# Chunk heads of a hybrid streaming encoder: one running minimum over both parts of the scores, and transposed probabilities laid out from a pair's first key block on

## Chip, cores and metric

One Trainium2 chip, one core. The metric is the device time of one execution in microseconds (us); several runs give a median. Engines: PE is TensorE, DVE is VectorE, ACT is ScalarE, POOL is GpSimd, SP is SyncE, whose queue here starts every transfer (DMA).

## What is computed

A step of two layers over 1024 prompt tokens and 64 sample tokens (T = 1088). Each layer normalizes the input, projects it, mixes tokens in three branches (latent attention with 8 heads, pooling, chunk attention with 4 heads), merges the branches, and applies an output projection and a gated side input. The change touches the chunk attention, whose core in the reference is:

```python
def ca_attend(q, k, v, q_pos, k_pos, rel_table):
    s = jnp.einsum("bnqhd,bnkhd->bnhqk", q, k).astype(jnp.float32) * CA_HEAD_DIM ** -0.5
...
    s = jnp.where(mask[None, :, None], s + bias[None], NEG_INF)
    pr = jax.nn.softmax(s, axis=-1).astype(v.dtype)
    return jnp.einsum("bnhqk,bnkhd->bnqhd", pr, v)
```

A query of a 64-token chunk sees its own chunk and the 8 before it, with a bias that depends on the distance.

## The kernel before

All matrices are multiplied in single precision split into a high and a low part (`mm3`: three matmuls for one product). Each layer runs in stages: projection (`gemm`, lines 349 to 395), attention (`attn_phase`, 759), a final merge (1423), output projection and gate (again `gemm`). The attention takes 12 heads in the order of `HEADS`: the 4 chunk heads, then the 8 latent heads. A head has 9 units, one for each block of 128 queries (`qb` 0 to 7 of the prompt, 8 is the sample). Chunk heads go through them in the order 8, 0, 1, ... 7.

`attention` (732) emits the units as a pipeline: scores of unit i, then the transposes, exponential, normalization and PV matmuls of earlier units. Beside them it emits filling work that needs nothing of the attention: `ple_proj` (1381; 16 steps a layer, each of which stores a tile `o` to `pp`), the pooling branch (1250) and `merge_bc` (1353; it loads the branch outputs `mbo` and `o`). A scheduler then sets the order of the instructions on each engine by its own estimate of when each is ready, so a shorter chain in one place moves the filling work of all engines and the transfers on SP's queue. Each engine runs its queue in that order.

A chunk unit (961) has up to 5 key blocks of 128. With over 512 score columns (`qb` 4 to 7: 640; the sample: 576) the scores are made in `nb = 2` parts, each in its own PSUM bank. One DVE instruction per part (line 986, shown in the profile as CUSTOM_DVE_ANT_0 with a DVE_READ_ACCUMULATOR2_ANT behind it, in the orders as ISA) adds the bias, negates, writes the result to `P` in SBUF and leaves the part's minimum in a column of `st`. `softmax` (796) then takes the minimum of both columns (line 803), ACT makes the exponential with it as its bias and the sum of the row (807), DVE the reciprocal (814) and POOL the multiplication (815). The latent units (1031) have their own minimum per part (1059) and use the same `softmax`, where the minimum of line 803 stays.

`transp` (832) transposes up to four blocks of `P` on PE into one PSUM bank and copies them into tiles `PT` of four key blocks, for a pair of query blocks: each copy (`split`) is an ACT cast (line 108) and a DVE subtraction (119). Before, the tile of key block b is `b // 4`, so a group of four transposed blocks that does not start at a multiple of 4 needs two copies. `weigh` (853) multiplies the values with them on PE (875; 867 for the sample).

Of the kernel before, what the change touches and what calls it, by code (L numbers as in the profile page):

```python
# [10 lines left out]
F32 = mybir.dt.float32  # L11
# [62 lines left out]
class K:  # L74
# [721 lines left out]
    def softmax(self, u, s, n, nb, st):  # L796

        nc = self.nc
        if not hasattr(u, "p"):
            u.p = self.sp.tile([128, 1024], F32, tag="P", name="P", bufs=NP)  # L800
        w = n // len(s)
        if nb == 2:
            nc.vector.tensor_tensor(st[:, 0:1], st[:, 0:1], st[:, 1:2], op=ALU.min)

        def exp():
            for c, x in enumerate(s):
                nc.scalar.activation(u.p[:, c * w:c * w + w], x, AF.Exp, bias=st[:, 0:1], scale=-1.0,  # L807
                                     accum_out=st[:, 2 + c:3 + c])
        u.exp = exp

        def norm():
            if len(s) == 2:
                nc.vector.tensor_add(st[:, 2:3], st[:, 2:3], st[:, 3:4])
            nc.vector.reciprocal(st[:, 4:5], st[:, 2:3])  # L814
            nc.gpsimd.tensor_scalar(u.p[:, :n], u.p[:, :n], st[:, 4:5], 1.0, op0=ALU.mult, op1=ALU.mult)  # L815
        u.norm = norm

    def unit(self, u, blocks, n, grp, qb, order, v, o, r0, z, dst):

        samp = qb == 8  # L820
        cols = [min(128 * i, n - 128) for i in range(len(blocks))]
        u.last = samp or qb % 2 == 1
        u.transposes = lambda i: self.transp(u.p, blocks[i:i + 4], cols[i:i + 4], grp, samp, qb % 2)

        def weigh():
            c0, w = (1024, 64) if samp else (256 * (qb // 2), 256)
            self.weigh(grp, v, o(), r0, c0, w)
            if r0:
                self.gated(o(), c0, w, qb // 2 == order[0] // 2, qb == order[-1], z, dst)
        u.weigh = weigh  # L830

    def transp(self, p, bb, cols, grp, samp, half):

        if not bb:
            return
        nc = self.nc
        w = 64 if samp else 128
        o = 0 if samp else 128 * half
        ps = self.pn.tile([128, 4, 128], F32, tag="n", name="pT")
        for j, c0 in enumerate(cols):  # L840
            nc.tensor.transpose(ps[:, j], p[:, c0:c0 + 128], self.ident)  # L841
        for b in bb:
            if b // 4 not in grp:
                grp[b // 4] = self.sp.tile([128, 4, 2, 256], F32R, tag="PT", name="PT", bufs=NPT)
            grp.setdefault("have", {}).setdefault(b, set()).add(half)
        j = 0
        while j < len(bb):
            m = min(len(bb) - j, 4 - bb[j] % 4)
            t = grp[bb[j] // 4][:, bb[j] % 4:bb[j] % 4 + m]
            self.split(ps[:, j:j + m, 128 - w:], t[:, :, 0, o:o + w], t[:, :, 1, o:o + w], "a", "v")  # L850
            j += m

    def weigh(self, grp, v, o, r0, c0, w):

        nc = self.nc
        have = grp["have"]
        if w == 256:
            for b, hs in have.items():
                if len(hs) == 1:
                    z = 128 * (1 - next(iter(hs)))  # L860
                    nc.gpsimd.memset(grp[b // 4][:, b % 4, :, z:z + 128].bitcast(F32), 0.0)
        ps = self.pv.tile([128, 512], F32, tag="v", name="pv")
        bl = sorted(have)
        t = self.sp.tile([128, 512], F32, tag="ot", name="ot", bufs=2)
        if w == 64:
            for i, b in enumerate(bl):
                nc.tensor.matmul(ps[:, :128].rearrange("p (j w) -> p j w", j=2), lhsT=v(b), rhs=grp[b // 4][:, b % 4, :, :w],
                                 start=i == 0, stop=i == len(bl) - 1)
            nc.scalar.copy(t[:64, :128], ps[64:, :128])
            nc.vector.tensor_add(t[:64, :128], ps[:64, :128], t[:64, :128])  # L870
            nc.vector.tensor_add(o[r0:r0 + 64, c0:c0 + w], t[:64, :64], t[:64, 64:128])
            return
        for i, b in enumerate(bl):
            for j in range(2):
                nc.tensor.matmul(ps[:, :w], lhsT=v(b), rhs=grp[b // 4][:, b % 4, j, :w], start=i + j == 0,  # L875
                                 stop=i == len(bl) - 1 and j == 1)
        self.npv = getattr(self, "npv", -1) + 1
        if PVE[self.npv % len(PVE)] == "v":
# [82 lines left out]
    def chunk_unit(self, p, h, qb, grp):  # L961
# [12 lines left out]
        def scores():  # L974
# [5 lines left out]
            for c in range(nb):  # L980
                ps = self.pg.tile([128, 512], F32, tag="s", name="S")
                cc = slice(c * w, c * w + w)
                for q in (q1, q2):
                    nc.tensor.matmul(ps[:, :w], lhsT=q[:, q0:q0 + 128], rhs=k[:, k0 + c * w:k0 + c * w + w],
                                     start=q is q1, stop=q is q2)
                nc.vector.tensor_tensor_reduce(out=u.p[:, cc], in0=ps[:, :w], in1=b[:, cc], op0=ALU.add, scale=-1.0,
                                               scalar=3e38, op1=ALU.min, accum_out=st[:, c:c + 1])
            self.softmax(u, [u.p[:, :n]], n, nb, st)
        u.scores = scores
        return u  # L990
# [642 lines left out]
```

## Time and profile before

| | |
|---|---|
| median of 3 runs | 2325.16 us |
| runs | 2326.8, 2313.66, 2325.16 us |
| profiled execution | 2322.09 us |
| its span, first to last instruction | 2320.2 us |
| instructions | 44847 |
| mean granted TensorE clock | 0.963 of full speed |
| chunk heads, layer 0 | about 590 to 697 us |
| chunk heads, layer 1 | about 1738 to 1846 us |

The span is one execution as the profiler saw it; the profiled execution's own time is 1.9 us longer. A row's time is the busy time of that group; "idle before" is how long the engine had nothing to do just before, with the one it waited for. The duration of an instruction is counted from where the engine takes it up, so two in a row can overlap in the records by some 0.07 us.

### The profile page before, as it was taken

The page shows a single profiled execution, that of the slowest core. Times are in us where ns is not written, and L with a number is a line of the kernel's source. Part 1 is how long each engine was busy: PE and PEld are TensorE (multiplying, and loading weights), DVE is VectorE, ACT ScalarE, POOL GpSimd, SP SyncE. Part 2 cuts the span into 40 slices and gives each one's busy share as a digit, 9 for nine tenths or more (in the row PEclk, how much of TensorE's full clock was granted, in tenths as well). Part 3 has the DMA queues.
Part 4 walks back from the last instruction along what each step waited for, and adds up shares of the span by engine and source line. Part 5 has one row for each costly group of instructions (what it writes and reads, how often), then busy time and mean ns, then how long its engine had stood idle before and what let it go on. Part 6 is the DMA issues. An engine that isn't in the chain of part 4 may idle for free.

```text
span 2320.2 us, 44847 instructions
## 1 busy us (share of the span) xinstructions
PE 2164.3 (93%) x16134; PEld 2081.4 (90%) x16134; DVE 1804.3 (78%) x3620; ACT 1211.6 (52%) x2549; POOL 908.8 (39%) x1048
## 2 busy tenths in 40 slices
PE   5999999999789999998979999999998899999988
PEld 4999999999688998998969999999987789999988
DVE  8566778766578888989996667877746788889898
ACT  6334355554577666345553343555546676654452
POOL 0444545576455554000004354447564565530000
PEclk8999999999899999998979999999998999999989
DMA  3533456454976764554634344453569666645353
GB/s 127 179 109 124 162 165 185 132 153 140 270 206 176 196 175 142 194 195 143 200 108 152 116 146 168 150 178 121 161 173 265 194 187 178 187 173 194 131 172 124
DMA packets 222193, 385.81 MB, mean 166 GB/s; under 512 B 30404, under 2 KB 114196, under 8 KB 221972
## 3 DMA queue, kind: packets, MB, share of 16 engines
q1 hardware_dynamic: 221972, 382.95, 52.8%
q8 instruction: 129, 2.11, 0.4%
q14 instruction: 92, 0.75, 0.1%
HBM read 248.16 MB, written 134.70 MB: 165 GB/s over the span
## 4 chain that ended last, share of the span: by engine, by line
PE 62%; DVE 15%; DMA 11%; issue 5%; ACT 4%; POOL 3%; SPq 1%; POOLq 0%; DVEq 0%; ACTq 0%
PE g L366 42%; PE S L1055 3%; DMA pp<-o 3%; PE pv L875 3%; PE pT L841 3%; DMA K<-bias_p 1%; DVE wop L119 1%; DMA g<-z 1%; PE mps L130 1%; PE mps L132 1%; PE mps L131 1%; SPq L85 1%; PE vps L1024 1%; DVE S L331 1%; PE turn L1100 1%
## 5 line engine op out<-in xcount | busy, mean ns | idle before, releaser
L108 ACT CAST wop<-wraw 128x512 fp32r<-128x512 f32 (+1 forms) x230 | 138.9, 606 | 266.0 <-PE g L366 171.3
L635 POOL TENSOR_TENSOR z<-z,rbc 128x544 f32<-128x544 f32 x134 | 206.7, 1547 | 180.9 <-DVE z L634 164.8
L815 POOL TENSOR_SCALAR P<-P,st 128x640 f32<-128x640 f32 (+8 forms) x216 | 155.3, 723 | 198.9 <-DVE st L814 116.6
L108 ACT CAST wop<-S 128x512 fp32r<-128x512 f32 x234 | 144.9, 619 | 165.8 <-PE g L366 163.8
L119 DVE TENSOR_TENSOR wop<-S,wop 128x512 fp32r<-128x512 f32 x194 | 170.1, 877 | 76.5 <-ACT wop L108 75.8
L119 DVE TENSOR_TENSOR PT<-pT,PT 128x512 fp32r<-128x512 f32 (+4 forms) x360 | 167.7, 473 | 47.5 <-ACT PT L108 45.4
L119 POOL TENSOR_TENSOR wop<-wraw,wop 128x512 fp32r<-128x512 f32 (+1 forms) x112 | 148.1, 1324 | 120.8 <-ACT wop L108 120.4
L366 PE MATMUL g<-T1h,wop 128*128 128x272 f32 x960 | 181.5, 301 | 14.2 <-DVE U L374 13.8
L366 PE MATMUL g<-B11h,wop 128*128 128x272 f32 x960 | 175.7, 293 | 18.1 <-ACT B11h L110 13.5
L366 PE MATMUL g<-T3h,wop 128*128 128x272 f32 x960 | 178.0, 294 | 13.3 <-ACT T3h L108 13.3
L366 PE MATMUL g<-T2h,wop 128*128 128x272 f32 x960 | 178.1, 295 | 5.6 <-ACT T2h L108 5.6
L366 PE MATMUL g<-B21h,wop 128*128 128x272 f32 x960 | 177.4, 295 | 5.8 <-ACT P L378 5.8
L108 ACT CAST PT<-pT 128x512 fp32r<-128x512 f32 (+4 forms) x360 | 147.1, 420 | 57.7 <-PE pT L841 50.6
L366 PE MATMUL g<-T4h,wop 128*128 128x272 f32 x960 | 173.8, 293 | 0.3 <-DVE U L374 0.3
L366 PE MATMUL g<-B22h,wop 128*128 128x272 f32 x960 | 172.9, 290 | 0.0
L875 PE MATMUL pv<-PT,V 128*128 128x256 f32 x928 | 167.6, 300 | 2.0 <-DVE PT L119 1.2
L1055 PE MATMUL S<-K,Q 96*128 96x384 f32 (+5 forms) x672 | 159.1, 353 | 7.5 <-ACT P L807 7.4
L366 PEld LDWEIGHTS g<-T1h,wop 128*128 128x128 f32 x960 | 148.5, 199 | 16.2 <-issue 13.8
L841 PE MATMUL pT<-ident,P 128*128 128x128 f32 x936 | 159.4, 280 | 2.8 <-DVE PT L119 1.5
L366 PEld LDWEIGHTS g<-B11h,wop 128*128 128x128 f32 x960 | 143.0, 192 | 20.5 <-ACT B11h L110 13.5
L130 PE MATMUL mps<-oh,wop 128*128 128x272 f32 x512 | 154.9, 304 | 5.6 <-ACT oh L108 3.2
L366 PEld LDWEIGHTS g<-T3h,wop 128*128 128x128 f32 x960 | 145.1, 193 | 15.6 <-ACT T3h L108 15.0
(269 smaller groups left out, 6509.0 us busy)
## 6 DMA issues: line engine op xcount, KB each, us to landing
wraw<-win SPq DMA_DIRECT2D x88, 512.0 KB
z<-z SPq DMA_DIRECT2D x96, 272.0 KB
g<-z SPq DMA_DIRECT2D x64, 272.0 KB
z<-z SPq DMA_DIRECT2D x24, 544.0 KB
Q<-q SPq DMA_DIRECT2D x32, 408.0 KB
K<-k SPq DMA_DIRECT2D x32, 400.0 KB
k<-hl SPq DMA_DIRECT2D x48, 256.0 KB
q<-hl SPq DMA_DIRECT2D x64, 192.0 KB
```

Of the source, the lines that this page charges most:

```text
L85: self.nc.sync.dma_start(out=self.raw(out), in_=self.raw(in_))
L108: nc.scalar.copy(out, src)
L119: e.tensor_sub(out, src, hi)
L130: mm(ps, lhsT=wh, rhs=xh, start=first, stop=False)
L131: mm(ps, lhsT=wh, rhs=xl, start=False, stop=False)
L132: mm(ps, lhsT=wl, rhs=xh, start=False, stop=last)
L366: nc.tensor.matmul(ps[:, c, :C], lhsT=hl[:, w, kb, :], rhs=b[:, kb, c * C:(c + 1) * C], start=k == 0 and not more, stop=k == 11, skip_grou ...
L635: nc.gpsimd.tensor_mul(o, o, self.half(self.r, ti))
L815: nc.gpsimd.tensor_scalar(u.p[:, :n], u.p[:, :n], st[:, 4:5], 1.0, op0=ALU.mult, op1=ALU.mult)
L841: nc.tensor.transpose(ps[:, j], p[:, c0:c0 + 128], self.ident)
L875: nc.tensor.matmul(ps[:, :w], lhsT=v(b), rhs=grp[b // 4][:, b % 4, j, :w], start=i + j == 0, stop=i == len(bl) - 1 and j == 1)
L1055: nc.tensor.matmul(ps[:, :ww], lhsT=q[0:96, q0:q0 + 128], rhs=k[0:96, k0 + c * w:k0 + c * w + ww], start=i == 0, stop=i == 2 and not diag)
```

## The change

In a chunk unit with two parts, the second part's reduction starts from the minimum of the first (a column of `st`, read as one number per partition) instead of from 3e38, and leaves the minimum of both in column 0. The separate minimum of line 803 stays for the latent units alone. And the tiles `PT` of a pair are counted from the first key block of the pair's first unit, with the groups of transposes cut so that each lies in one tile. The core of the diff:

```diff
@@ softmax
-        if nb == 2:
+        if len(s) == 2:
             nc.vector.tensor_tensor(st[:, 0:1], st[:, 0:1], st[:, 1:2], op=ALU.min)
@@ unit
-        u.transposes = lambda i: self.transp(u.p, blocks[i:i + 4], cols[i:i + 4], grp, samp, qb % 2)
+        m = grp.setdefault("first", blocks[0])
+        k = min(4, 4 - (blocks[0] - m) % 4)
+        u.transposes = lambda i: self.transp(u.p, *((x[k:] if i else x[:k]) for x in (blocks, cols)), grp, samp, qb % 2)
@@ transp
+        m = grp["first"]
         for b in bb:
-            if b // 4 not in grp:
-                grp[b // 4] = self.sp.tile([128, 4, 2, 256], F32R, tag="PT", name="PT", bufs=NPT)
+            if (b - m) // 4 not in grp:
+                grp[(b - m) // 4] = self.sp.tile([128, 4, 2, 256], F32R, tag="PT", name="PT", bufs=NPT)
...
         while j < len(bb):
-            m = min(len(bb) - j, 4 - bb[j] % 4)
-            t = grp[bb[j] // 4][:, bb[j] % 4:bb[j] % 4 + m]
-            self.split(ps[:, j:j + m, 128 - w:], t[:, :, 0, o:o + w], t[:, :, 1, o:o + w], "a", "v")
-            j += m
+            i = (bb[j] - m) % 4
+            k = min(len(bb) - j, 4 - i)
+            t = grp[(bb[j] - m) // 4][:, i:i + k]
+            self.split(ps[:, j:j + k, 128 - w:], t[:, :, 0, o:o + w], t[:, :, 1, o:o + w], "a", "v")
+            j += k
@@ weigh
-        have = grp["have"]
+        have, m = grp["have"], grp["first"]
+
+        def at(b):
+            return grp[(b - m) // 4][:, (b - m) % 4]
...
@@ chunk_unit
                 nc.vector.tensor_tensor_reduce(out=u.p[:, cc], in0=ps[:, :w], in1=b[:, cc], op0=ALU.add, scale=-1.0,
-                                               scalar=3e38, op1=ALU.min, accum_out=st[:, c:c + 1])
+                                               scalar=st[:, 1:2] if c else 3e38, op1=ALU.min,
+                                               accum_out=st[:, 1:2] if c < nb - 1 else st[:, 0:1])
```

Elsewhere in `weigh` the tiles are looked up by `at(b)`; nothing else changes. Latent heads begin with key block 0 in every unit of the prompt, so their groups stay as they were. Lines from 824 on move down by up to 9.

DVE, layer 0, the last units of the first chunk head (`ISA P,st` is the reduction of line 986, `ISA st` its accumulator read, `S` the scores, `K` the bias in a tile of that name). Before:

```order
L986 ISA P,st<-S,K_6856 128x320
L986 ISA st 128x1
L986 ISA P,st<-S,K_6856 128x320
L986 ISA st 128x1
L119 TENSOR_TENSOR PT<-pT,PT 128x4x128
L814 RECIPROCAL st<-st 128x1
L803 TENSOR_TENSOR st<-st 128x1
```

and now:

```order
L994 ISA P,st<-S,K_6856 128x320
L994 ISA st 128x1
L814 RECIPROCAL st<-st 128x1
L888 TENSOR_TENSOR o<-pv,ot 64x256
L119 TENSOR_TENSOR PT<-pT,PT 128x4x128
L994 ISA P,st<-S,K_6856,st 128x320
L994 ISA st 128x1
```

The second reduction now names `st` as an input, stands behind three other instructions, and nothing of line 803 follows it. It waits for DVE's own semaphore of the first part, as line 803 did.

ACT, layer 0, copies of transposed probabilities between the second and the third chunk head (`PT<-pT` is the cast, `o<-pps` a copy of `ple_proj`, `ot<-pv` one of the PV output). Before:

```order
L108 CAST PT<-pT 128x128 x2
L807 ACTIVATE P,st<-P,st 128x128
L1394 COPY o<-pps 128x272
L108 CAST PT<-pT 128x2x128
L879 COPY ot<-pv 64x256
L108 CAST PT<-pT 128x128
L108 CAST PT<-pT 128x2x128
```

and now:

```order
L108 CAST PT<-pT 128x2x128
L807 ACTIVATE P,st<-P,st 128x128
L1403 COPY o<-pps 128x272
L108 CAST PT<-pT 128x4x128
L887 COPY ot<-pv 64x256
L108 CAST PT<-pT 128x128
```

Two casts of one block became one of two, and two of two blocks one of four.

SP, layer 0, transfers before the last chunk head (`pp<-o` is a store of `ple_proj`, `V<-vc` a load of values). Before:

```order
L85 DMA wraw<-wpp 128x2x128
L85 DMA pp_107<-o 128x544
L85 DMA V<-vc_125 128x1664
```

and now:

```order
L85 DMA wraw<-wpp 128x2x128
L85 DMA V<-vc_125 128x1664
L85 DMA pp_107<-o 128x544
```

The store stands behind the load. Further on, among the first latent heads, the store `mbo<-po` and the loads `of<-mbo` and `of<-o` of `merge_bc` stand some places later than before.

## Rows read from the trace of the kernel before

**Rows 1.** The page, part 1: busy time, share of span, instructions of each engine.

```profile
PE 2164.3 (93%) x16134; PEld 2081.4 (90%) x16134; DVE 1804.3 (78%) x3620; ACT 1211.6 (52%) x2549; POOL 908.8 (39%) x1048
```

**Rows 2.** Stretches: length, busy PE, PEld, DVE, ACT, POOL (instructions); clock, DMA share, GB/s.

```profile
590.00:697.00 107.00, 88.20 (x571) 78.86 (x571) 73.09 (x262) 70.05 (x199) 54.30 (x86) 0.90 0.84 233
697.00:740.00 43.00, 37.61 (x255) 32.29 (x254) 34.25 (x97) 30.12 (x87) 25.50 (x34) 0.99 0.77 219
740.00:950.00 210.00, 206.47 (x1576) 193.22 (x1575) 178.93 (x483) 131.51 (x373) 93.64 (x133) 0.99 0.58 170
...
1738.00:1846.00 108.00, 87.19 (x567) 77.97 (x568) 73.21 (x262) 71.14 (x201) 54.19 (x86) 0.90 0.83 232
```

**Rows 3.** Chain of waits within 590 to 697 us, then 1738 to 1846 us, by line.

```profile
by line: DMA pp<-o 35.4%; DMA K<-bias_p 13.8%; DMA of<-p 6.1%; SPq L85 5.6%; PE pv L875 4.7%; PE S L984 4.5%; PE pps L130 4.2%; PE pT L841 3.8%; DVE P L986 3.2%; PE pps L131 2.7%; PE pps L132 2.6%; issue 2.6%; PE vps L1024 2.5%; DVE st L803
...
by line: DMA pp<-o 27.0%; DMA K<-bias_p 8.5%; DMA z<-z 5.4%; PE pT L841 5.2%; DMA pu<-z 5.0%; PE pv L875 4.9%; DVE P L986 4.9%; PE S L984 4.7%; PE pps L130 4.2%; issue 3.8%; SPq L85 3.2%; PE pps L131 3.1%; PE pps L132 3.0%; PE vps L1024 2.5
```

**Rows 4.** ACT's waits, the same two stretches: us in total, times, longest.

```profile
ACT o L1394 <- DMA pp<-o: 10.2, 4, 3.3
...
ACT P L807 <- DVE st L803: 3.9, 3, 2.0
...
ACT o L1394 <- DMA pp<-o: 14.2, 5, 6.5
ACT P L807 <- DVE st L803: 4.5, 4, 1.9
```

**Rows 5.** Line 803: both stretches (length, DVE busy), then all 120, ns min/median/max.

```profile
590.00:697.00 107.00, 6.78 (x19) 0.90 0.84 233
1738.00:1846.00 108.00, 6.63 (x19) 0.90 0.83 232
...
L803 DVE TENSOR_TENSOR st<-st x120: 128/154/1790, 598.7 to 2059.8; 128x1 f32<-128x1 f32 x120
```

**Rows 6.** In order of time, DVE, then POOL: start, duration in us.

```profile
660.84 0.08 DVE L986 DVE_READ_ACCUMULATOR2_ANT st<- 128x1 f32 x1
660.84 0.49 DVE L986 CUSTOM_DVE_ANT_0 P<-S,K 128x320 f32<-128x320 f32 x1
...
661.92 1.79 DVE L803 TENSOR_TENSOR st<-st 128x1 f32<-128x1 f32 x1
...
661.87 0.73 POOL L891 TENSOR_TENSOR o<-o,acc 128x256 f32<-128x256 f32 x1
662.57 1.11 POOL L1275 TENSOR_TENSOR pb<-pa 128x560 f32<-128x560 f32 x1
```

**Rows 7.** In order of time, DVE, line 803 without POOL in its way.

```profile
635.66 0.15 DVE L803 TENSOR_TENSOR st<-st 128x1 f32<-128x1 f32 x1
635.73 0.15 DVE L814 RECIPROCAL st<-st 128x1 f32<-128x1 f32 x1
```

**Rows 8.** Line 1107 (ns min/median/max), one instance in time, POOL beside it.

```profile
L1107 DVE SCALAR_TENSOR_TENSOR hl<-turn,gh,hl x26: 471/736/751, 330.6 to 1542.0; 128x512 fp32r<-128x512 f32 x24, 128x256 fp32r<-128x256 f32 x2
...
333.76 0.73 DVE L1107 SCALAR_TENSOR_TENSOR hl<-turn,gh,hl 128x512 fp32r<-128x512 f32 x1
...
333.31 1.36 POOL L635 TENSOR_TENSOR z<-z,rbc 128x544 f32<-128x544 f32 x1 [3.94 <-DVE z L634]
```

**Rows 9.** Copies of transposed probabilities, 590 to 697 us: busy us, mean ns, idle before.

```profile
L119 DVE TENSOR_TENSOR PT<-pT,PT 128x128 fp32r<-128x128 f32 x22 | 5.7, 281 | 1.4 <-ACT PT L108 1.4
L119 DVE TENSOR_TENSOR PT<-pT,PT 128x384 fp32r<-128x384 f32 x10 | 5.5, 550 | 0.6 <-ACT PT L108 0.4
...
L108 ACT CAST PT<-pT 128x128 fp32r<-128x128 f32 x22 | 5.2, 265 | 0.4
L108 ACT CAST PT<-pT 128x384 fp32r<-128x384 f32 x10 | 4.7, 472 | 1.3 <-PE pT L841 1.3
```

**Rows 10.** Transfers issued from 590 to 700 us: the loads of values, size each.

```profile
V<-vc SPq DMA_DIRECT2D x4, 832.0 KB
```

More of the change, by code (lines that the diff above doesn't have):

```diff
@@ L860, in weigh @@
                     z = 128 * (1 - next(iter(hs)))
-                    nc.gpsimd.memset(grp[b // 4][:, b % 4, :, z:z + 128].bitcast(F32), 0.0)
+                    nc.gpsimd.memset(at(b)[:, :, z:z + 128].bitcast(F32), 0.0)
         ps = self.pv.tile([128, 512], F32, tag="v", name="pv")
@@ L866, in weigh @@
             for i, b in enumerate(bl):
-                nc.tensor.matmul(ps[:, :128].rearrange("p (j w) -> p j w", j=2), lhsT=v(b), rhs=grp[b // 4][:, b % 4, :, :w],
+                nc.tensor.matmul(ps[:, :128].rearrange("p (j w) -> p j w", j=2), lhsT=v(b), rhs=at(b)[:, :, :w],
                                  start=i == 0, stop=i == len(bl) - 1)
@@ L874, in weigh @@
             for j in range(2):
-                nc.tensor.matmul(ps[:, :w], lhsT=v(b), rhs=grp[b // 4][:, b % 4, j, :w], start=i + j == 0,
+                nc.tensor.matmul(ps[:, :w], lhsT=v(b), rhs=at(b)[:, j, :w], start=i + j == 0,
                                  stop=i == len(bl) - 1 and j == 1)
```

## Prediction

> **What bounds the kernel now.** I read the page's busy shares first, then the busy time by stretch, then the chain of waits, then the groups of one stretch, and last single instructions in order of time. The reader is to see first that PE is busy for 93% of the span [rows 1], so a saving on another engine counts only where PE waits for it. By stretch [rows 2] there are two kinds of place. From 740 to 950 us PE is busy 206.5 of 210 us: nothing that DVE or ACT saves there ends earlier. In the chunk heads, 590 to 697 us in the first layer and 1738 to 1846 us in the second, PE is busy only 88.2 of 107 us and 87.2 of 108 us, DVE 73 us and ACT 70 to 71 us. The change edits work of these two stretches alone, 215 us of 2320 us. What PE waits for there is in the chain [rows 3]: in layer 0 the landings of three transfers (stores of pp 35.4%, loads of the bias 13.8%, loads of p 6.1%) make 55.3%, in layer 1 four of them (27.0, 8.5, 5.4 and 5.0%) make 45.9%. So about half of each stretch, 50.6% on the mean, hangs on transfers, whose bytes the change leaves alone. ACT waited 10.2 and 14.2 us for pp stores, and 3.9 and 4.5 us for the small minimum of line 803 [rows 4].
>
> **The change, part by part.**
>
> (a) The small minimum of line 803 goes from the 40 chunk units whose scores have two parts (5 of 9 units, 4 heads, 2 layers). In the two stretches it took 6.78 + 6.63 = 13.41 us of DVE [rows 5], and 38 of the 40 lie there: 0.353 us each, against a median of 0.154 us over all 120 of its kind. It does nearly nothing, so the rest must be waiting inside the instruction. The time order shows one: it starts at 661.92 us and lasts 1.79 us, until 663.71 us, while POOL runs from 661.87 to 663.68 us in two instructions that read SBUF [rows 6]. The Trainium skill, "SBUF — State Buffer", section "Who interferes with whom", says that a VectorE instruction with two SBUF inputs contends with a GpSimd instruction that reads SBUF, and the loser blocks; this row agrees. What counts is not DVE's 13.4 us but ACT's wait of 3.9 + 4.5 = 8.4 us, since DVE has spare time in the stretch. I take 8.4; the ends are 0 and 13.4 us.
>
> (b) In its place the second part's reduction waits for the first part's accumulator, 40 times. Before, the second part started at 660.84 us with the accumulator read of the first: no gap [rows 6]. A wait on an accumulator just written shows where line 803 ran undisturbed: it began at 635.66 us and the next instruction at 635.73 us, so it took 0.07 us of the queue, 0.15 us by its own row [rows 7]. I take 0.07: 40 x 0.07 = 2.8 us; the ends are 0 (the new order puts another instruction between most halves) and 40 x 0.15 = 6.0 us. Behind the waiting reduction stand DVE's splits of transposed probabilities, for which the PV matmuls wait. The Trainium skill, "VectorE: DVE Perf Modes", section "The DRAIN you can't avoid", says that such a same-engine read needs a semaphore and that the semaphore costs nothing extra; by it this term would be 0 and the time 1.4 us lower. No run here shows it yet. Could the new reduction be held behind POOL as line 803 was? It reads scores from PSUM, the bias from SBUF and a per-partition number. The nearest row is line 1107, which also reads PSUM, SBUF and such a number: at 333.76 us it took 0.73 us while POOL read SBUF from 333.31 to 334.67 us, and its range over 26 is narrow, 751 ns at most against a median of 736 [rows 8]. So I take no hold; the end is the 0.353 - 0.154 = 0.199 us of (a), 40 times, 8.0 us.
>
> (c) Query blocks 5, 6 and 7 of each chunk head split their transposed probabilities in two copies in place of three: 24 ACT casts and 24 DVE subtractions go, the elements stay. ACT took 265 ns for 128 columns and 472 for 384, so 103 per 128 columns and 162 fixed; DVE 281 and 550, so 135 and 146 fixed [rows 9]. That is 24 x 0.162 = 3.9 us of ACT and 24 x 0.146 = 3.5 us of DVE. One follows the other on one path and they overlap with neighbours, so I take ACT's 3.9; the ends are 0 and 7.4 us. Transposes and PV matmuls keep their number.
>
> Together (a) to (c) are -8.4 + 2.8 - 3.9 = -9.5 us. With 50.6% of the stretch on transfers, 0.494 of it is left: -4.7 us.
>
> (d) PE's order moves. Filling matmuls (ple_proj, merge_bc) slide later: behind the last PV of the attention stood 384 matmuls of mm3 in a row, now 420, so 36 per layer leave the attention, 15 of them the chunk stretch and 21 the start of the latent heads. One takes about 206.47 us / 1576 = 0.131 us where PE is full [rows 2]. Where PE is full this costs nothing: the work comes later and what stood behind it earlier. Where PE has holes, the hole grows by their idle share: 1 - 88.2/107 = 17.6% in the chunk stretch and 1 - 37.6/43 = 12.5% from 697 to 740 us [rows 2]. 15 x 0.131 x 0.176 + 21 x 0.131 x 0.125 = 0.69 us, twice 1.4 us. The ends are 0 and 36 x 0.131 x 2 = 9.4 us.
>
> (e) SP's order moves one pp store behind a load of values. That load is 832 KB [rows 10]; at the 233 GB/s of the stretch [rows 2] it takes 852 / 233 = 3.7 us, 7.3 us in two layers. ACT waited for a pp store 4 + 5 = 9 times [rows 4] for 32 stores, so I take 9/32 of it: 2.1 us; the ends are 0 and 7.3 us. The operands of merge_bc (mbo, o) are also loaded later, by a few transfers; its price lies within (d).
>
> The sum is -4.7 + 1.4 + 2.1 = -1.2 us. The profiled execution took 2322.09 us, 2320.2 of span and 1.9 around it; it becomes 2320.9. It lay 3.07 us under the median of the runs shown (2325.16), so as a median I forecast 2324.0 us. A measurement of this kernel can tell about 1%, 23 us, from no change: the forecast is no change.
>
> **The rivals.**
>
> First, the stretch is not held by its transfers but by DVE and ACT, which feed the copies that stand in ACT's queue before the next store. Then all that was saved counts: -13.4 - 3.9 - 3.5 + 2.8 = -18.0 us, 2304.1 on the profile's base, 2307.2 as a median. For it: ACT's waits for line 803 are up to 2 us long and in front of the copies; against it: DMA share 0.84 and 0.83 over the whole stretch [rows 2].
>
> Second, on the slower side: the transfers hold the chunk stretch for all of its length, nothing of (a) to (c) is seen, and the 36 matmuls that left the attention in each layer are missed there, because PE finds nothing else to do. Each then costs its full 0.131 us behind the attention, where PE is full anyway: +9.4 us, 2331.5, as a median 2334.6. It decides as soon as the time from the first chunk score to the last latent score shrinks by less than the 36 x 0.131 = 4.7 us of matmuls taken out of it in a layer. For it: PE idles 18.8 and 20.8 us in the two stretches; against it: from 740 us on PE has hardly a hole.
>
> Third, the change doesn't do what it says: the second reduction, with its number from SBUF, is held behind POOL just as line 803 was. 8.0 us come back, (-9.5 + 8.0) x 0.494 + 1.4 + 2.1 = +2.8 us, 2324.9, as a median 2328.0. The rows of line 1107 speak against it.
>
> **How the numbers follow.** Forecast 0.55, first rival 0.22, second 0.18, third 0.05. Cases of both signs hold most of the chance, so the likeliest one's own range stands beside: 2317 to 2331 us. The range for 8 in 10 reaches to the first rival's time below and the second's above, 2308 to 2336. Faster by over 1% (under 2302) asks for the first rival and more, a quarter of its chance: 0.06. Slower by over 1% (over 2348) asks for the second with all of (e) and holes that spread, a fifth of it: 0.04. Within 1%: 0.90.
>
> **What would show it.** In the profile after: DVE's time on line 803's kind is gone from the chunk stretches and the second reductions stay near 0.48 us (wrong if some take 1 us or more beside POOL). ACT waits there for the reduction itself, under 3 us per layer in place of 3.9 and 4.5. The splits count 24 fewer on ACT and on DVE. The chunk stretches are 1 to 3 us shorter each, with pp stores still about half of their chain; were they 6 us or more shorter, the first rival is right. PE's busy time in the first 40 us of the latent heads falls by 1 to 2 us per layer; if the attention as a whole is not shorter and the time is up by some 9 us, the second rival is.

## The result and the profile after

The changed kernel takes 2346.53 us as the median of 6 runs (2339.23 to 2353.96), the kernel before 2324.53 us beside it: a ratio of 1.0104, with a 95% interval of 1.0082 to 1.0127. It is slower by 22 us, and the predicted 2324.0 us with its range of 2308 to 2336 misses it.

The profiled execution took 2353.96 us, the longest of the six, with a span of 2352.2 us against 2320.2 before. Busy time by engine, from the page, answers to [rows 1]:

```profile
PE 2176.1 (93%) x16134; PEld 2089.0 (89%) x16134; DVE 1797.6 (76%) x3556; ACT 1209.5 (51%) x2525; POOL 908.5 (39%) x1048
```

DVE has 64 instructions fewer (40 small minima, 24 subtractions) and ACT 24 casts fewer, PE the same number. The work that was to go has gone. Next the stretches of the changed kernel, as in [rows 2]: chunk heads of layer 0, first latent heads, the other latent heads up to their last score, the tail from there to the next `gemm`, and the chunk heads of layer 1.

```profile
587.00:694.00 107.00, 84.68 (x551) 75.97 (x550) 66.08 (x232) 69.09 (x187) 53.05 (x85) 0.90 0.84 232
694.00:740.00 46.00, 41.48 (x290) 36.42 (x289) 35.90 (x100) 32.96 (x94) 24.47 (x36) 0.98 0.76 211
740.00:915.00 175.00, 168.49 (x1258) 155.47 (x1259) 146.58 (x416) 114.78 (x336) 89.92 (x126) 0.99 0.59 164
915.00:987.00 72.00, 65.98 (x493) 63.29 (x493) 56.32 (x98) 23.39 (x47) 7.68 (x10) 0.98 0.50 172
1756.00:1861.00 105.00, 85.49 (x553) 76.92 (x552) 66.21 (x232) 69.37 (x187) 53.50 (x85) 0.91 0.84 236
```

The same two stretches of layer 0 in the kernel before, from 740 us to the last latent score and from there to the next `gemm`:

```profile
740.00:913.00 173.00, 169.96 (x1294) 158.01 (x1293) 148.63 (x425) 115.62 (x339) 86.44 (x124) 0.99 0.59 167
913.00:972.00 59.00, 58.51 (x459) 57.22 (x458) 52.30 (x94) 22.96 (x47) 7.20 (x9) 1.00 0.54 188
```

The reader is to see two things. From 740 us on PE does 36 matmuls fewer (1258 against 1294), yet the stretch lasts 175 us and not 173: its idle time rose from 3.0 to 6.5 us. And the tail grew from 59 to 72 us, with 34 matmuls more and 6.0 us of idle PE in place of 0.5. The tail is the loss. Counted from the last latent score to the first `gemm` matmul behind it, with the filling and merge matmuls alone (`mps`) and the granted clock, both layers of the kernel before:

```profile
913.10:971.60 58.50, 52.67 (x408) 1.00 0.54 187
2058.70:2116.90 58.20, 52.62 (x408) 1.00 0.52 183
```

and of the changed kernel:

```profile
914.60:986.50 71.90, 60.36 (x444) 0.98 0.50 170
2079.10:2149.30 70.20, 59.08 (x444) 1.00 0.50 169
```

That is 13.4 + 12.0 = 25.4 us of the 32.0 us between the two spans. The `gemm` stages make up most of the rest (from the first to the last of their matmuls between the two attentions 765.1 us against 758.9; the other runs below, whose `gemm` is the same, have 759.7 to 767.4), and the attention up to its last score is about as long in the two profiles: from the first chunk score to the last latent score 327.7 and 323.0 us, against 327.3 and 323.6.

Now the tail itself. The chain of waits of the changed kernel, layer 0, from the last PV on (start, duration, what):

```profile
924.96 0.38 ACT ot L887
...
925.81 0.45 DVE g L1383
926.26 0.04 issue
926.30 0.39 PE mps L130
...
927.36 0.45 DVE g L1383
927.81 0.04 issue
927.85 0.40 PE mps L130
...
932.56 0.39 PE mps L130
...
933.61 0.63 ACT wop L108
934.26 1.84 DVE wop L119
936.12 0.55 SPq L85
...
937.90 6.75 DMA g<-z
...
944.77 0.73 DVE g L1463
...
945.55 0.40 PE mps L130
```

Six groups of `merge_bc` (6 matmuls each) run behind the last PV, one every 1.55 us (the first at 924.76 us by PE's own records, then 926.30, 927.85 and so on to 932.56): six matmuls, then the DVE multiplication of line 1383 that empties the bank, then the next six. `merge_bc` has one PSUM bank, so nothing overlaps. The wait table of the same tail says it too:

```profile
PE mps L130 <- DVE g L1383: 3.3, 6, 0.6
PE mps L130 <- DVE g L1463: 2.1, 1, 2.1
```

Behind the last group follow a cast of weights (its buffer was held by `merge_bc`), the weight load and, behind it on SP's queue, the first gate row `g<-z` of the final merge, which by the pools of the code takes memory that `merge_bc` held. It lands at 944.65 us, PE stands for its bank (2.1 us), and then the granted clock is lower:

```profile
940.00:950.00 10.00, 7.89 (x51) 7.67 (x50) 5.12 (x8) 1.26 (x2) 0.00 (x0) 0.83 0.88 338
```

In the kernel before, the same chain from the last multiplication of `merge_bc` (line 1374 there) ran beside transposes, PV matmuls and the first matmuls of the final merge:

```profile
921.57 0.36 DVE g L1374
...
921.99 1.92 POOL g L1376
...
925.39 5.92 DMA g<-z
...
931.41 0.33 DVE g L1454
```

There PE waited 0.3 us for that bank:

```profile
PE mps L130 <- DVE g L1454: 0.3, 1, 0.3
```

Counted from the last latent score, the first multiplication of the final merge now comes 11.9 us later (944.77 - 914.60 = 30.2 us behind it, against 931.41 - 913.10 = 18.3 us), and the next `gemm` 13.4 us later.

### The profile page after: what moved, and what is told of

Read it like the earlier page. It is cut to its first block, busy times and chain, and to the rows that moved or that the text cites. A ratio compares the mean times of both kernels' runs of the same rounds, so it can differ in the third digit from the quotient of the medians.

```text
span 2352.2 us, 44771 instructions
## 1 busy us (share of the span) xinstructions
PE 2176.1 (93%) x16134; PEld 2089.0 (89%) x16134; DVE 1797.6 (76%) x3556; ACT 1209.5 (51%) x2525; POOL 908.5 (39%) x1048
## 4 chain that ended last, share of the span: by engine, by line
PE 59%; DVE 16%; DMA 12%; issue 5%; ACT 4%; POOL 3%; SPq 1%; DVEq 0%; POOLq 0%; ACTq 0%
PE g L366 39%; PE S L1064 3%; PE pv L883 3%; DMA pp<-o 3%; PE pT L843 3%; DMA g<-z 2%; PE mps L130 2%; DVE wop L119 2%; DMA Q<-qc 1%; PE mps L132 1%; PE mps L131 1%; DMA of<-o 1%; SPq L85 1%; DVE S L331 1%; PE turn L1109 1%
## 5 line engine op out<-in xcount | busy, mean ns | idle before, releaser
L119 DVE TENSOR_TENSOR PT<-pT,PT 128x512 fp32r<-128x512 f32 (+3 forms) x336 | 164.5, 496 | 37.7 <-ACT PT L108 35.0
L108 ACT CAST PT<-pT 128x512 fp32r<-128x512 f32 (+3 forms) x336 | 143.8, 439 | 51.8 <-PE pT L843 44.8
L366 PEld LDWEIGHTS g<-T3h,wop 128*128 128x128 f32 x960 | 144.9, 193 | 15.4 <-ACT T3h L108 14.5
```

Source lines behind the costliest of these rows:

```text
L108: nc.scalar.copy(out, src)
L119: e.tensor_sub(out, src, hi)
L366: nc.tensor.matmul(ps[:, c, :C], lhsT=hl[:, w, kb, :], rhs=b[:, kb, c * C:(c + 1) * C], start=k == 0 and not more, stop=k == 11, skip_grou ...
```

## The experiments

All ratios are to the kernel before on the same chip; the tail is measured as above, from the profile of each run, and the last column is the time from the first chunk score to the last latent score. Pairs are layers 0 and 1. The last column is of one execution each and weak evidence in layer 0: three kernels with the same order of work on PE, DVE, ACT and POOL up to the last score (after; weight split on POOL; six groups left out) show 327.7, 324.3 and 317.7 us there, and 323.0, 323.0 and 322.3 us in layer 1.

| run | median us | ratio, 95% interval | `mps` behind the last score | tail us | up to the last score us |
|---|---|---|---|---|---|
| before | 2324.53 | 1 | 408, 408 | 58.5, 58.2 | 327.3, 323.6 |
| after | 2346.53 | 1.0104 (1.0082 to 1.0127) | 444, 444 | 71.9, 70.2 | 327.7, 323.0 |
| minimum alone | 2345.21 | 1.0091 (1.0069 to 1.0114) | 426, 444 | 64.5, 69.6 | 326.7, 325.6 |
| layout alone | 2349.78 | 1.0111 (1.0086 to 1.0136) | 426, 426 | 64.5, 65.2 | 332.9, 329.6 |
| both, filling begun earlier | 2338.68 | 1.0064 (1.0043 to 1.0085) | 444, 444 | 71.7, 70.3 | 322.7, 317.4 |
| before, filling begun earlier | 2327.36 | 1.0017 (0.9999 to 1.0036) | 402, 402 | 58.5, 58.2 | 328.2, 324.8 |
| before, pooling held back | 2358.36 | 1.0153 (1.0131 to 1.0174) | 450, 450 | 70.8, 72.4 | 331.2, 326.0 |
| both, shared bank (transposes) | 2449.86 | 1.0552 (1.0528 to 1.0576) | 384, 384 | 58.0, 60.2 | 388.9, 387.3 |
| before, shared bank (transposes) | 2454.96 | 1.0574 (1.0550 to 1.0598) | 384, 384 | 59.5, 60.2 | 385.9, 391.0 |
| both, weight split on POOL | 2345.42 | 1.0099 (1.0076 to 1.0121) | 444, 444 | 69.1, 70.7 | 324.3, 323.0 |
| both, shared bank (values), last half step | 2374.90 | 1.0217 (1.0199 to 1.0235) | 384, 384 | 60.2, 57.9 | 349.2, 347.0 |
| before, the same | 2356.55 | 1.0125 (1.0101 to 1.0149) | 384, 384 | 58.0, 59.8 | 339.7, 339.0 |
| both, early gate row | 2338.40 | 1.0057 (1.0042 to 1.0073) | 444, 444 | 69.2, 69.4 | 321.3, 322.5 |
| both, six groups left out | 2324.99 | 1.0014 (0.9994 to 1.0034) | 408, 408 | 63.9, 62.5 | 317.7, 322.3 |
| before, six groups left out | 2325.10 | 1.0005 (0.9986 to 1.0024) | 384, 384 | 60.4, 61.3 | 328.1, 324.4 |
| both, two banks of its own | 2431.41 | 1.0458 (1.0428 to 1.0487) | 384, 384 | 59.0, 59.6 | 378.9, 380.1 |

### Each half of the change alone

```diff
 # minimum alone: only this of the change
-        if nb == 2:
+        if len(s) == 2:
...
-   scalar=3e38, op1=ALU.min, accum_out=st[:, c:c + 1])
+   scalar=st[:, 1:2] if c else 3e38, op1=ALU.min,
+   accum_out=st[:, 1:2] if c < nb - 1 else st[:, 0:1])
```

> The running minimum alone, the layout as before. In the order of PE 402 matmuls stand in a row behind the last PV matmuls of the attention, 18 of them merge_bc's (384 before, 420 with both edits). Theory T (tail): the loss is made behind the last PV matmuls, where the left-over matmuls of merge_bc drain through one PSUM bank and hold up what the final merge needs; it goes by their number, so half the loss: ratio to before near 1.005 (+11 us), the stretch from the last latent score to the next projection near 65 us (58.5 before, 71.9 with both edits). Theory E (the edit's own work): the minimum's wait on its own engine makes the loss: ratio 1.010 and chunk stretches that are not shorter. Or the layout makes it: ratio 1.000 or under.

```diff
 # layout alone: all the rest of the change, the minimum as before
+            if (b - m) // 4 not in grp:
+                grp[(b - m) // 4] = self.sp.tile([128, 4, 2, 256], F32R, tag="PT", name="PT", bufs=NPT)
...
```

> The layout of the transposed probabilities alone, the minimum as before. 402 matmuls in a row behind the last PV, 18 of them merge_bc's. Theory T: half the loss, ratio near 1.005, stretch behind the last latent score near 65 us. Theory E: all of the loss (1.010) or none (1.000 or under), according to which edit carries it; the two alone then differ.

Measured: 1.0091 and 1.0111, each as slow as both together, where the theory of the tail had half the loss for each. The edits' own work in the chunk heads doesn't explain it, for these did not become longer: from the first chunk score to the first latent score 108.8 and 107.2 us with the minimum alone, 102.3 and 102.5 with the layout alone, 109.5 and 109.6 before. What the two runs share is a longer tail. The minimum alone leaves 426 matmuls behind the last score in layer 0 and 444 in layer 1, as its trace counts them:

```profile
909.20:973.70 64.50, 55.68 (x426) 1.00 0.53 185
2069.50:2139.10 69.60, 59.03 (x444) 1.00 0.49 169
```

So within one kernel the layer with 18 more matmuls behind the attention has a tail 5.1 us longer. Over the runs with this kernel's banks and all of its filling: 402 and 408 go with 58.2 to 58.5 us, 426 with 64.5 to 65.2, 444 and 450 with 69.1 to 72.4. That is some 6 us for each 18 matmuls, 0.34 us each, where PE needs 0.131 [rows 2]. The layout alone loses about half elsewhere: its attention up to the last score is also 5.6 and 6.0 us longer, and that lies in the latent heads (first to last latent score 230.6 and 227.1 us, against 217.9 and 214.0 before). No run gives the cause.

### Filling begun earlier

```diff
-NEAR, BESIDE = 8, 14
+NEAR, BESIDE = 8, 20
```

> Both edits, and the filling work handed to the scheduler 20 units before the end of the attention in place of 14; this leaves no matmul of merge_bc behind the last PV (384 in a row, as before the change). Theory T: the loss is gone, ratio 0.996 to 1.000, the stretch behind the last latent score back near 58 us. Theory E: the edits are all there, so the loss stays: ratio 1.008 to 1.012.

> Control: the kernel before with the same 20 in place of 14; 384 in a row behind the last PV as before. Both theories: ratio 0.998 to 1.002. If it is itself faster by 1%, the run with both edits and 20 says nothing on the edits.

Measured: this edit was a poor lever. In the changed kernel it leaves 444 behind the last score all the same (384 in a row was expected), and the tail stayed at 71.7 and 70.3 us; the time fell to 1.0064, and what is shorter in its profile is the attention, 322.7 and 317.4 us, for which no run gives the cause. On the kernel before it changes nothing that can be told (1.0017). Starting the filling sooner doesn't decide what is left over at its end.

### The kernel before with work left over

```diff
     def beside(self, l):
         g = self.bg
         while g:
-            g = [x for x in g if next(x, self) is not self]
+            turn = getattr(self, 'turn_', 0)
+            self.turn_ = turn + 1
+            g = [x for x in g if (turn % 2 and x is self.bg[1] and len(g) == 2) or next(x, self) is not self]
```

> Neither edit. The pooling branch, whose output merge_bc waits for, gets every second turn of the filling work, so merge_bc starts later: 450 matmuls of merge_bc and merge behind the last latent score, 426 of them in a row behind the last PV (408 and 384 before, 444 and 420 with both edits). Theory T (the left-over matmuls behind the last PV): as slow as with both edits, the stretch from the last latent score to the next projection 70 to 74 us, ratio 1.008 to 1.014. Theory E (the edits' own work makes the loss): 58 us and ratio 0.998 to 1.003.

Measured: 1.0153, with 450 matmuls behind the last score and tails of 70.8 and 72.4 us. This kernel has none of the change in it, only its filling in another order. So a left-over makes the long tail without the change. The ratio lies above the 1.008 to 1.014 of the theory: it is 12 us slower than the changed kernel, and its attention is longer too (331.2 and 326.0 us), so the tail is not all that it pays.

### More banks for the filling

```diff
-                    ps = self.po.tile([128, 512], F32, tag="o", name="mps")
+                    ps = self.pn.tile([128, 512], F32, tag="n", name="mps") if c else self.po.tile([128, 512], F32, tag="o", name="mps")
```

> Both edits; every second group of merge_bc takes its PSUM bank from the pool of the transposes, so merge_bc has two banks in turn in place of one and runs ahead: 384 matmuls behind the last latent score, none of merge_bc. Theory T: the loss is gone, the stretch behind the last score 52 to 58 us, ratio 0.990 to 1.000. Theory E: ratio 1.006 to 1.012.

> Neither edit, merge_bc on two banks as in the run with both edits: 384 behind the last score here too. The run with both edits against this one is the price of the edits with the left-over taken out: theory T 0.997 to 1.001, theory E 1.006 to 1.012. Against the kernel before: 0.992 to 1.003.

Measured: 1.0552 and 1.0574, a miss. Nothing is left over and the tails are back at 58.0 to 60.2 us, but a bank shared with the transposes has to be used in the order of the program, so nearly all of `merge_bc` stands in one lump before the last heads. There the attention waits for the filling; this is the first of the two kernels:

```profile
890.00:940.00 50.00, 35.90 (x232) 32.76 (x231) 19.01 (x40) 3.12 (x6) 17.46 (x14) 0.93 0.58 182
```

ACT, which makes the exponentials, is busy 3.12 of 50 us. What the pair does show: where both kernels have the same lump and no left-over, the changed one is not the slower (2449.86 against 2454.96 us), as the theory of the tail had it for the pair.

The weight cast in ACT's queue, on which the loads of the final merge wait, was tried next, with the splits of one weight block moved to POOL:

```diff
...
-        self.woa[m] = self.weights(self.d["woa"][l, m], 4, "v")
+        self.woa[m] = self.weights(self.d["woa"][l, m], 4, *(("g", "g") if m == 4 else ("v",)))
```

> Both edits, left-over as with them (444 and 420). The split of the final merge's second weight tile, whose cast waits in ACT's queue until merge_bc gives a weight buffer back, goes to POOL, which is idle there; so ACT's casts of the last branch output, which stood behind it, come some 8 us earlier. If that queue is what makes the left-over cost more than its matmuls: stretch behind the last score 60 to 66 us, ratio 1.002 to 1.007. If the matmuls on their single bank are all of it: 70 to 73 us and ratio 1.008 to 1.012.

Measured: 1.0099, tails of 69.1 and 70.7 us: no gain. The six groups of 1.55 us stood there as before and the next weight block's cast took the place of the moved one.

Then a bank of the PV outputs, for the last half step of `merge_bc` alone:

```diff
-                    ps = self.po.tile([128, 512], F32, tag="o", name="mps")
+                    ps = self.pv.tile([128, 512], F32, tag="v", name="mps") if m == 7 and ti and c else self.po.tile([128, 512], F32, tag="o", name="mps")
```

> The changed kernel, in which merge_bc's last two groups of one half take their PSUM bank from the pool of the PV outputs instead of its own single bank. By the instruction order no filling matmul is then left behind the last PV beyond the 384 of the final merge, and the filling up to the last sixth of the latent heads stands as in the changed kernel; the moved groups stand in that last sixth (60 and 90 instead of 48 and 42 filling matmuls in its halves, and none behind). Theory (the left-over filling work behind the attention makes the loss): the stretch from the last latent score to the next gemm falls from 71.9 and 70.2 us to the 58 to 59 us of the kernel before; the latent heads grow by the 36 matmuls moved back, 36 x 0.131 = 4.7 us, and somewhat more where PV outputs wait for the shared bank; in all 2346 - 2 x (12.5 - 4.7) = 2331 us, between 2322 and 2340. Rival (the loss comes from the chunk heads or the splits themselves): the time stays at 2346 us although nothing is left over.

> The kernel before with the same edit of merge_bc's bank as the run of the changed kernel beside it: a control. In the order 384 matmuls stand behind the last PV, as in the kernel before, so theory and rival both expect a tail of 58 to 59 us; what the time differs from 2324 us is the price of the shared bank alone. Theory: between 2320 and 2330 us, and the changed kernel with this edit is within 6 us of it, since the change then has no left-over to pay for. Rival: the changed kernel with the edit is still 20 us or more above this one.

Measured: 1.0217 and 1.0125. The tails are 57.9 to 60.2 us as both theories had it for the control and the theory for the changed kernel, but the times are far above what the theory gave, and the two kernels stand 18 us apart, not within 6. The surplus was not gone. It had moved into the last sixth of the latent heads, which holds 150 filling matmuls in the changed kernel and 108 in the control, against 90 and 84 without the edit. At 1.55 us for each six, 42 more are 7 x 1.55 = 10.9 us per layer, near the 9.5 and 8.0 us by which that attention is longer than the control's. That is worked out, not tried by itself, and it is not all: the control took in 24 matmuls and its attention is 12.4 and 15.4 us longer than that of the kernel before, more than 4 x 1.55 us, so the shared bank has a price of its own.

Last, two banks of its own for the filling, with one fewer for the scores:

```diff
-         "attn": (("pg", 3), ("pn", 2), ("po", 1), ("pv", 2))}
+         "attn": (("pg", 2), ("pn", 2), ("po", 2), ("pv", 2))}
```

> The changed kernel with two PSUM banks of its own for the filling work and two instead of three for the scores. By the order nothing is left over (384 behind the last PV), but the filling runs out after two thirds of the latent heads. Theory: the tail falls to 58 to 60 us, while PE has nothing to fill the last third of the latent heads (some 70 us) with, where it is idle about a tenth to a fifth of the time: -25 + 7 to 14, 2328 to 2335 us if the scores do with two banks. Rival (two banks for the scores hold the pipeline): 2346 us or more, with longer waits of PE for the banks of the scores in the whole attention.

Measured: 1.0458, the rival. The filling was used up early, and from 700 to 960 us PE waited far longer for the banks of the scores, 16.0 us in 16 waits against 3.5 us in 6 in the changed kernel up to 915 us. These 12.5 us are a part of the 51 us by which that attention is longer; what the rest waits for is not shown.

```profile
PE S L1064 <- ACT P L807: 16.0, 16, 2.5
```

### The gate row of the final merge loaded early

```diff
...
     def last_pairs(self, l):
+        self.zt = self.at("Z0", H, "g", F32)
+        self.ld(self.zt, self.z_d[l][Z_MIX][:, :H])
...
-                nc.vector.tensor_tensor(self.half(g, ti), self.half(g, ti), ps[:, :, :C], op=ALU.mult)
+                gt = self.zt.rearrange("p (c x) -> p c x", c=2) if m + ti == 0 else self.half(g, ti)
+                nc.vector.tensor_tensor(gt, gt, ps[:, :, :C], op=ALU.mult)
```

> The changed kernel, in which the first half of the first gate row of the final merge (a load g<-z) has an SBUF tile of its own and is loaded before the attention ends, so that the first DVE multiplication of the final merge waits neither for memory of merge_bc nor for the loads of weights on SP's queue. The order on PE is that of the changed kernel (420 in a row behind the last PV). Theory of the chain (of the 12 to 13 us of tail per layer the larger part is a chain behind the last merge_bc group: POOL addition, SP, load of the gate row, DVE, PE's bank): the 11.2 us from 933.6 to 944.8 us are covered by 24 more matmuls, 3 us per layer, perhaps 1 us more since PE's clock does not dip: 2346 - 6 to - 8 = 2338 to 2340 us, tail 67 to 68 us; the six groups of 1.55 us stay. Rival (the tail is paid by the six groups alone, one bank at a time): no change, 2346 us, tail 70 to 72 us.

Measured: 2338.40 us, 1.0057, inside what the chain theory gave. Behind the six groups PE stands 0.6 us for its bank in place of 2.1, and its clock does not fall; its stretch behind them reads

```profile
930.00:940.00 10.00, 10.00 (x80) 9.85 (x79) 5.91 (x10) 2.54 (x4) 0.00 (x0) 1.00 0.81 301
```

But the tails fell only to 69.2 and 69.4 us, by 2.7 and 0.8 us. So the late gate row is the smaller part of the tail, the six groups the larger. The rest of the 8 us is not in the tail and has no shown cause. Unlike what was expected, this edit also changed PE's order inside the attention (filling matmuls among the first chunk units stand elsewhere), so it does not test the gate row alone.

### The left-over left out

These two kernels leave out the same six groups of `merge_bc` in each layer, 36 matmuls and six DVE multiplications.

```diff
             for g, b in zip(gs, (0, 2)):
+                if m == 7 and ti + b > 0:
+                    continue
```

> The changed kernel without the last six groups of merge_bc in each layer (36 matmuls and six DVE multiplications left out: the last output row block gets only one of its eight partial products). By the order these are exactly the 36 that stood behind the last PV: 384 are left in a row, 408 behind the last latent score, and the filling inside the attention is that of the changed kernel, twelfth by twelfth. Theory (the six groups behind the attention pay 4.6 us of matmuls, 4.7 us of waits for the single bank, and 2 to 4 us through the late gate row): the tail falls from 71.9 and 70.2 us to 58 to 60 us, the time from 2346 to 2320 us, 2314 to 2326. Rival one (the matmuls count at full rate only, as the second rival of the prediction had it): 2346 - 9.4 = 2337 us. Rival two (the loss stands elsewhere): 2342 us or more.

> The kernel before without the same six groups of merge_bc in each layer. There they stand among the last latent heads, and 384 matmuls are behind the last PV with or without them. Theory (inside the attention these groups fill PE's holes and cost at most their own time): the time falls by 0 to 36 x 0.131 x 2 = 9.4 us, to 2315 to 2325 us, with the tail at 58 us; the price of the same groups behind the attention, by the run beside it, is then two to three times as large. Rival (they cost as much where they stand before): 2300 us.

Measured: 1.0014 (0.9994 to 1.0034) for the changed kernel, 1.0005 (0.9986 to 1.0024) for the kernel before. This pair shows what the place costs. The same 36 matmuls per layer cost the kernel before nothing that can be told (by the interval at most 3 us), where they stand between the last scores, transposes and PV matmuls, and the changed kernel (1.0104 - 1.0014) x 2324 = 21 us, give or take 7 by the two intervals, where they stand behind them. Without them the two kernels take the same time. The expected tail was off: 63.9 and 62.5 us, not 58 to 60, since the filling still ends late. In layer 0 PE waits for the bank that is emptied with the gate row, in layer 1 2.0 us for a cast of `oh`; the wait of layer 0:

```profile
PE mps L130 <- DVE g L1465: 3.8, 1, 3.8
```

Against the changed kernel the tail is 8.0 and 7.7 us shorter, 15.7 of the 21 us. The other 5 us cannot be placed: in the profile the attention of layer 0 is 10.0 us shorter with the same order of work, which is the spread told above the table.

## Why the prediction was wrong, point by point

**(a), (b), (c): the mechanisms held.** No minimum of line 803 stands in the chunk stretches, where [rows 5] had 38; the 80 that are left begin with the latent heads. Second reductions of the changed kernel and line 803 (ns min/median/max), and between them second and first reductions of one shape in the chunk stretch of layer 0 (busy us, mean ns):

```profile
L994 DVE CUSTOM_DVE_ANT_0 P<-S,K,st x40: 500/535/553, 598.5 to 1861.8; 128x320 f32<-128x320 f32 x32, 128x288 f32<-128x288 f32 x8
...
L994 DVE CUSTOM_DVE_ANT_0 P<-S,K,st 128x320 f32<-128x320 f32 x15 | 8.0, 537 | 0.1
L994 DVE CUSTOM_DVE_ANT_0 P<-S,K 128x320 f32<-128x320 f32 x15 | 7.2, 481 | 0.8 <-PE pT L843 0.7
...
L803 DVE TENSOR_TENSOR st<-st x80: 131/151/1299, 701.3 to 2080.1; 128x1 f32<-128x1 f32 x80
```

Of one shape, a second reduction takes 537 ns against 481, 0.06 us more, where (b) took 0.07. None of the 40 exceeds 553 ns, although POOL was busy for more than half of the time of 26 of them, so POOL holds none and the third rival falls. That the extra 0.06 us is the wait on the semaphore and not the number read from SBUF, no run separates; the Trainium skill's "costs nothing extra" ("VectorE: DVE Perf Modes", section "The DRAIN you can't avoid"), said there of copies, would have it 0 and isn't borne out by these rows as they stand. ACT's waits in the two chunk stretches, as in [rows 4]:

```profile
ACT o L1403 <- DMA pp<-o: 13.4, 4, 4.0
...
ACT P L807 <- DVE st L994: 1.2, 4, 0.4
...
ACT o L1403 <- DMA pp<-o: 12.6, 4, 4.1
...
ACT P L807 <- DVE st L994: 1.3, 4, 0.4
```

ACT waits 2.5 us for the reductions where it waited 8.4 us for line 803. In the chunk stretch of layer 0 the casts of one block went from 22 [rows 9] to 10, and those of four blocks at once from 7 to 10:

```profile
L108 ACT CAST PT<-pT 128x512 fp32r<-128x512 f32 x10 | 5.8, 590 | 1.1 <-PE pT L843 1.0
...
L108 ACT CAST PT<-pT 128x128 fp32r<-128x128 f32 x10 | 2.6, 263 | 0.3 <-PE pT L843 0.2
```

The chunk stretches, from their first score to the first latent score, became 1.4 and 3.8 us shorter, about the 1 to 3 us that were forecast; the two other profiles with the same order (weight split on POOL; six groups left out) have 1.8 and 6.6 us in layer 0 and 5.1 and 3.1 us in layer 1. None of it is left in the time of the whole: with the left-over out, the two kernels differ by 0.0009 x 2324 = 2 us, less than their intervals, and there the tails of the changed kernel are still 3.5 and 1.2 us longer than those of the other.

**The transfers.** They were to stay about half of the chain of the chunk heads. In the changed kernel those named make 64 and 66% of it, more than the 55.3 and 45.9% of [rows 3]:

```profile
by line: DMA pp<-o 30.4%; DMA K<-kc 12.3%; DMA ckf<-ckv_c 10.4%; DMA Q<-qc 6.2%; DMA pu<-z 5.1%; SPq L85 3.8%; PE pps L130 3.6%; PE pT L843 3.6%; PE S L992 3.2%; issue 3.0%; PE pv L883 3.0%; ACT P L807 3.0%; PE vps L1033 2.5%; PE pps L131 2
...
by line: DMA pp<-o 31.4%; DMA ckf<-ckv_c 9.7%; DMA K<-kc 8.8%; DMA z<-z 5.9%; DMA Q<-qc 5.5%; DMA pu<-z 5.1%; PE pT L843 4.1%; PE pps L130 3.4%; PE S L992 3.3%; PE pv L883 3.2%; issue 3.1%; PE pps L131 2.4%; SPq L85 2.2%; PE pps L132 2.1%; 
```

So with the engines' part cut, the transfers hold the stretch for more of its length. (The stores of `pp` alone, which the signs put at about half, are 30.4 and 31.4%, after 35.4 and 27.0%.) The first rival (all savings count) asked for chunk stretches 6 us or more shorter; of the six values above one is, and the time went the other way.

**(e) was near.** ACT waited 13.4 + 12.6 = 26.0 us for the stores of `pp`, 1.6 us more than the 24.4 of [rows 4]; 2.1 was taken.

**(d) is the step that failed.** It saw the 36 matmuls per layer go behind the attention and priced them at 1.4 us, by the sentence "Where PE is full this costs nothing: the work comes later and what stood behind it earlier." The first half is so: in the first third of the latent heads PE did 60 `merge_bc` matmuls per layer against 96, and 264 from there to the last score in both kernels, so what was missed early was never caught up. The second half is not so: from the first to the last latent score the changed kernel takes 219.6 and 217.2 us against 217.9 and 214.0, and the two other profiles with its order 214.8 to 218.5. In the kernel before these groups stood in holes, where taking them out frees nothing that can be told (1.0005). The sign set for (d), PE's busy time falling by 1 to 2 us in the first 40 us of the latent heads, did not come either: 17 more matmuls of `ple_proj` slid in there for 15 of `merge_bc`. Layer 0 before, then after:

```profile
695.30:735.30 40.00, 36.65 (x251) 31.40 (x251) 33.41 (x95) 28.70 (x85) 23.78 (x34) 1.00 0.79 223
...
695.00:735.00 40.00, 36.89 (x262) 32.21 (x259) 32.57 (x89) 27.59 (x80) 20.99 (x31) 1.00 0.79 214
```

The upper end of (d), 9.4 us, was wrong in its unit price. 0.131 us is the price of a matmul where PE has other work beside it. Alone, behind the attention, six `merge_bc` matmuls take 1.55 us, 0.26 us each, because they and the DVE multiplication share one bank: 6 x 1.55 = 9.3 us per layer, twice the 4.7. Then the start of the final merge slips with them: in layer 0 another 2.1 us of waiting and 10 x (1 - 0.83) = 1.7 us at the lower clock, together 13.1 of the 13.4 us of the tail; in layer 1 waits of 1.3 us for a cast of `oh` and 0.5 us for the bank, together 11.1 of the 12.0 us.

**The second rival had the place and the sign.** Its condition (a shrinkage of less than 4.7 us per layer) is met in the profile of the changed kernel (0.4 us longer and 0.6 shorter) and in five of the six values of the three profiles with that order, and 36 matmuls per layer are missed in the attention and paid behind it. Its first half, that nothing of (a) to (c) is seen in the chunk heads, is not so. It came out 12 us short, 2334.6 against 2346.53 us, most of it by the same unit price (2 x 9.3 = 18.6 us in place of 9.4). It had a chance of 0.18; what was held against it, that PE has hardly a hole from 740 us on, should have weighed less, because a hole that filling work closes looks like a full engine.

What stays open: why the layout alone lengthens the latent heads, where the 8 us of the early gate row come from beyond the 3.5 us in the tails, why one order of work takes 317.7 to 327.7 us in layer 0, and how to spread the surplus again. That the single bank sets the price of 1.55 us is read from the waits; the runs with more banks changed too much else to show it alone. No version that was run beats the kernel before.

## What to carry to other kernels

Work that fills holes is free only while it stands beside other work: price a matmul that a new order leaves over by how it runs alone (here one PSUM bank, so six matmuls, an emptying, six matmuls), and then by what waits for its buffers. An engine that shows 98% busy may be busy with filling, and taking that out makes a hole, not a gain. When an edit of a few small instructions moves a scheduler's order, count what stands behind the last critical instruction before and after, and run both kernels once with exactly that surplus left out.

## What the runs showed of the hardware

The clock of PE fell in the tail when PE had been waiting. In layer 0 of the changed kernel it stood for the gate row's bank until 945.55 us, and shortly after, its matmuls came every 0.23 us in place of 0.13, in the chain at 946.63 and 946.86 us:

```profile
946.32 0.12 PE mps L131
946.45 0.18 PE mps L132
946.63 0.23 PE mps L130
946.86 0.23 PE mps L131
```

The granted clock of that stretch was 0.83 (the row from 940 to 950 us above), a mean over the two levels of 1.2 and 2.4 GHz; with the gate row early, PE waited 0.6 us there and the clock was 1.00. In layer 1 of the changed kernel PE waited 1.3 and 0.5 us in the tail, and the clock of the whole tail was 1.00. The kernel with the left-over cut out shows the same dip behind its wait of 3.8 us:

```profile
925.00:935.00 10.00, 7.17 (x46) 7.17 (x47) 7.21 (x12) 2.46 (x4) 0.00 (x0) 0.83 0.87 337
```
